# A decoder layer's second MLP product with its operands prepared two pairs to an instruction, and work moved between the vector engines

## The chip, the cores and the metric

The kernel runs on one core of a Trainium2 chip. The metric is the device time of one execution in microseconds. The core's engines are TensorE (PE in the profile; its weight loads are PEld), VectorE (DVE), ScalarE (ACT), GpSimd (POOL) and SyncE (SP), which here only issues transfers. Each takes its instructions in order and waits on semaphores for the others.

## The reference

One hybrid decoder layer, for 2048 tokens of width 1024, in float32:

```python
h = rmsnorm(x, g_mix);  z = h @ w_in
y_a = rwkv7_mix(token_shift(z[..., :RWKV_COLS]), ...) @ w_out_a
y_b = multiscale_pool_mix(z_pool, ...) @ w_out_b
x = x + (sigmoid(gA) * y_a + sigmoid(gB) * y_b) @ w_o
h = rmsnorm(x, g_mlp)
x = x + square(relu(h @ w_ff1)) @ w_ff2            # 1024 -> 4096 -> 1024
h = rmsnorm(x, g_ple)
x = x + sigmoid(h @ w_ple_gate) * (p @ w_ple_proj)
out = rmsnorm(x, g_final)
```

## The kernel before

The stages follow one another: the mixing stage (0 to 1690 us of the profile), the MLP's first product (1690 to 2390), its second (2390 to 3037), and the gate stage (3037 to the end).

A float32 operand is split for TensorE (`split`): ScalarE casts it to a rounded form, the high part, and DVE or POOL subtracts that from it, which leaves the low part. A product of two split operands is three matmuls (`mm3`: high by high, high by low, low by high). Each matmul is 128x128 by 128x512.

Both MLP products work on two blocks of 1024 tokens and replace eight products of half-size operands by seven, P1 to P7, of sums and differences of the halves (a Strassen scheme in Winograd's form). The activations' combinations (A11, S2, A12, S3, S1, A22, S4) are kept as `home` operands on chip in the first product, and go through DRAM (`rD`) in between.

The first product runs over two blocks and 16 pairs of hidden blocks. `pair` is one of these: its seven products have the order P1, P6, P2, P7, P5, P4, P3, and DVE, POOL and ScalarE form the results and their relu squared in the `t2` ring (7 tiles; L1276, L1282). Between P7 and P5, `combine` prepares the next pair's weights (lines 1165 to 1192). While block 0 runs, `heads1` norms block 1's tokens, in four groups of two tiles: ScalarE's sum of squares (L160, with an output nobody reads, a junk tile of the `t2` ring), a reciprocal root by an integer guess and Newton steps on DVE (L149 to L155, operations on 128x1), the scaling on DVE (L173, `hr`), transposes on TensorE (L137), and the home operands of block 1 into DRAM. As the last pair of block 0 finishes with each home operand, `fill_home` reads block 1's in its place.

The second product runs over `seq`: two blocks, four chunks of four pairs each, seven products in the order P1, P2, P5, P6, P7, P4, P3. One product is 48 matmuls, about 11 us. While it runs, `operands` prepares the next: the activations `raw` from DRAM in one transfer of 1 MB, split pair by pair with the low parts on POOL, and the weights (`w2`, in place combinations for P5, P6, P7 and P4 on POOL, split with the low parts on DVE). Operand tiles come from one ring: 16 tiles, two products' worth. Each product's results are added from PSUM into accumulators `accs` (ScalarE copies the first, L1440; DVE adds the others, L1442); in a block's last chunk DVE forms the outputs from them (L1448, L1460), and they are stored to `x2D`. At the block's first chunk the accumulators P2, P4 and P3 start from `x1D`.

The gate stage begins with the split of its weights (`weights`, tiles `wg`). Its first two tokens' norms (`norm_in`) are in the program near the end of the second product; the scheduler puts them where their rows are ready.

TensorE's order is written by hand. The order on the other engines is the scheduler's, from priorities that follow the program's order. SP's queue carries nearly all transfers.

## Time and profile before

| | us |
|---|---|
| median of 3 runs | 3304.99 (3300.75 to 3310.25) |
| the profiled execution | 3303.2 |
| its span | 3301.4 |
| mean granted clock of TensorE | 0.967 |
| TensorE busy | 3054.8 (93%) |
| VectorE busy | 2455.9 (74%) |
| GpSimd busy | 1653.8 (50%) |
| ScalarE busy | 1336.2 (40%) |

A busy engine is not always the one that sets the end; what matters is what it waited for. In the rows of the trace, `a<-b` is output from input, the time in brackets is TensorE's idle time before the instruction with the engine, tile and line that ended it, and a row with `x24 | 30.4, 1275 |` has a count, a busy time in us and a mean in ns.

### The profile page before, as it was taken

To read this page: it belongs to the slowest core of one execution; us is meant where nothing else is said; L and a number is where in the kernel's file an instruction comes from. 1 tells how busy PE (TensorE), PEld (TensorE's weight loads), DVE (VectorE), ACT (ScalarE), POOL (GpSimd) and SP (SyncE) were. 2 spreads that over 40 slices of the span, in tenths; PEclk is the share of its full clock that TensorE was granted. 3 is DMA by queue.
4 is the path that set the end of the run, shared out by engine and by line. 5 is a ranking of instruction groups with operands and counts; after the bars stand their busy time and mean duration, and the time that the engine had idled before them with its cause. 6 is when DMAs were issued, how large, how long until landed. Compare 5 with 4: busy or idle time off the path is not lost. (4 is left out here: it accounts for less than half of the span.)

```text
span 3301.4 us, 44294 instructions
## 1 busy us (share of the span) xinstructions
PE 3054.8 (93%) x14409; PEld 2492.0 (75%) x14409; DVE 2455.9 (74%) x5424; ACT 1336.2 (40%) x2774; POOL 1653.8 (50%) x1657
## 2 busy tenths in 40 slices
PE   7999989999999998788989889899989998999998
PEld 6777777777878786677777667688878886887787
DVE  4479888788888878875477777776657697668665
ACT  4445655455455444432233223222244434443332
POOL 4545444444334434531245456655589887885000
PEclk9999999999999999899999999899999999999999
DMA  7876767765666567767755455544464464335331
GB/s 246 241 225 196 244 202 233 237 216 192 216 211 218 188 205 238 246 213 264 273 193 177 148 177 190 181 153 147 169 227 153 142 217 177 141 128 177 127 115 67
DMA packets 423219, 636.41 MB, mean 193 GB/s; under 512 B 174222, under 2 KB 286412, under 8 KB 391756
## 3 DMA queue, kind: packets, MB, share of 16 engines
q1 hardware_dynamic: 420684, 629.39, 57.7%
q10 hardware_dynamic: 2304, 4.20, 0.3%
q8 instruction: 114, 1.87, 0.2%
q14 instruction: 117, 0.96, 0.1%
HBM read 439.49 MB, written 193.99 MB: 192 GB/s over the span
## 5 line engine op out<-in xcount | busy, mean ns | idle before, releaser
L133 PE MATMUL d<-big,wf 128*128 128x512 f32 (+1 forms) x3288 | 849.7, 406 | 19.1 <-DVE wf L244 8.9
L133 PEld LDWEIGHTS d<-big,wf 128*128 128x128 f32 x3288 | 609.5, 192 | 157.7 <-DVE wf L244 11.4
L1103 DVE TENSOR_TENSOR op<-w,op 128x512 fp32r<-128x512 f32 x224 | 287.4, 1295 | 139.2 <-ACT op L1102 137.8
L1103 POOL TENSOR_TENSOR op<-hr,op 128x512 fp32r<-128x512 f32 x224 | 331.2, 1494 | 95.5 <-ACT op L1102 95.5
L133 PE MATMUL d<-op 128*128 128x512 f32 x1344 | 314.6, 393 | 12.6 <-POOL op L1103 8.9
L133 PEld LDWEIGHTS d<-op 128*128 128x128 f32 x1344 | 253.4, 189 | 69.2 <-POOL op L1103 9.3
L1102 ACT CAST op<-hr 128x512 fp32r<-128x512 f32 x224 | 139.3, 622 | 323.2 <-PE rc L133 109.8
L872 DVE TENSOR_TENSOR Xtmp<-Xt,At 128x16 f32<-128x16 f32 (+15 forms) x512 | 242.8, 474 | 9.3
L1103 POOL TENSOR_TENSOR op<-wr,op 128x512 fp32r<-128x512 f32 x96 | 141.5, 1483 | 206.3 <-ACT op L1102 206.3
L133 PE MATMUL d<-yx,wf 128*128 128x512 f32 x768 | 206.9, 416 | 22.7 <-ACT yx L390 15.7
L133 PE MATMUL d<-wf,big 128*128 128x512 f32 x768 | 200.8, 415 | 26.1 <-DVE t2k L611 13.8
L133 PE MATMUL d<-wg,op 128*128 128x512 f32 x768 | 187.0, 399 | 11.3 <-ACT wg L1102 11.0
L133 PEld LDWEIGHTS d<-wf,big 128*128 128x128 f32 x768 | 146.6, 196 | 64.1 <-DVE t2k L611 17.4
L1276 POOL TENSOR_TENSOR t<-t,t 128x512 f32<-128x512 f32 x128 | 189.4, 1490 | 9.8 <-issue 5.6
L133 PEld LDWEIGHTS d<-yx,wf 128*128 128x128 f32 x768 | 147.3, 198 | 59.8 <-ACT yx L390 17.4
L133 PE MATMUL rp<-op 128*128 128x512 f32 x672 | 173.5, 393 | 13.9 <-DVE accP L1442 12.3
L133 PEld LDWEIGHTS d<-wg,op 128*128 128x128 f32 x768 | 147.1, 192 | 46.4 <-ACT wg L1102 11.6
L1102 ACT CAST op<-wr 128x512 fp32r<-128x512 f32 x192 | 110.0, 618 | 166.9 <-DMA wr<-in_w_ff_dram 113.1
L133 PE MATMUL rc<-op 128*128 128x512 f32 x672 | 171.7, 391 | 0.0
L244 POOL TENSOR_TENSOR wf<-wr,wf 128x640 fp32r<-128x640 f32 (+2 forms) x69 | 120.5, 1747 | 78.5 <-ACT wf L241 74.3
L133 PEld LDWEIGHTS rp<-op 128*128 128x128 f32 x672 | 126.9, 190 | 42.0 <-issue 12.7
L875 DVE TENSOR_REDUCE Xt<-Xtmp 128x8 f32<-128x16 f32 (+15 forms) x512 | 147.3, 288 | 9.2
(319 smaller groups left out, 6396.4 us busy)
## 6 DMA issues: line engine op xcount, KB each, us to landing
wf<-wc SPq DMA_DIRECT2D x131, 1024.0 KB, 5.4
wc<-wf SPq DMA_DIRECT2D x50, 1024.0 KB, 6.3
wr<-in_w_ff_dram SPq DMA_DIRECT2D x64, 512.0 KB, 4.4
w<-in_w_ff_dram SPq DMA_DIRECT2D x64, 512.0 KB, 4.2
wr<-in_w_in_dram SPq DMA_DIRECT2D x51, 512.0 KB, 4.3
zD<-t2k SPq DMA_DIRECT2D x96, 256.0 KB, 3.9
zs<-zD SPq DMA_DIRECT2D x32, 640.0 KB, 6.4
At<-aD SPq DMA_DIRECT2D x32, 512.0 KB, 5.1
```

The lines of the kernel that those rows point to most:

```text
L133: PE.matmul(out_, lhsT, rhs, start=start, stop=stop, **kw)
L244: eng.tensor_tensor(wf[:, 1, c], raw[:, c], hi.bitcast(F32)[:, c], ALU.subtract)
L872: DVE.tensor_tensor(tmp[:, :, :, 0:n], Xt[:, :, 0:n].unsqueeze(2).broadcast_to([P, MCOL, FS, n]), At[:, 0:n, r:n].rearrange("p s r -> p r ...
L875: DVE.tensor_reduce(Xt[:, :, r:n].unsqueeze(3), tmp[:, :, :, 0:n], AX.X, ALU.add)
L1102: ACT.copy(out=dst[0], in_=src)
L1103: eng.tensor_tensor(dst[1], src, dst[0].bitcast(F32), ALU.subtract)
L1276: eng.tensor_tensor(out_, a, b, op)
```

## The change

- The operand ring has tiles of twice the size, half as many. In the first product each is handed out in halves (`ophalf`).
- In the second product two pairs share an instruction: two casts and two low parts for the activations of a product instead of four each, two and two for the weights. Of the activations' low parts the first stays on POOL and the second is DVE's. The weight combinations go from POOL to DVE. The weights come in transfers of 1 MB instead of 512 KB.
- In the first product P7's weight difference goes from POOL to DVE.
- Block 1's norms take their squares in halves of 512 into a tile of their own, with an added 128x1 sum on DVE; the other norms are as before.
- `fill_home` gets high priority, and its low parts are 1024 and 512 wide on DVE and 512 wide on POOL instead of 1024 on each.
- P4's and P3's accumulators are loaded at P6 instead of P1; the last block's stores go from ScalarE's queue to SP's; the gate stage's first two weight transfers are issued one product before the end.

```diff
--- before.py
+++ after.py
@@ -1085,15 +1085,24 @@
             return t
 
         gb = gvec(g_mlp[0])
-        ring = dict(n=0, a=6, b=6)
+        ring = dict(n=0, a=3, b=3)
 
         def optile():
 
             n = ring["n"] % (ring["a"] + ring["b"])
             ring["n"] += 1
             if n < ring["a"]:
-                return hx.tile([P, 2, 512], FR, name="op", tag="op", bufs=ring["a"])
-            return ring["pool"].tile([P, 2, 512], FR, name="op", tag="op", bufs=ring["b"])
+                return hx.tile([P, 2, 2, 512], FR, name="op", tag="op", bufs=ring["a"])
+            return ring["pool"].tile([P, 2, 2, 512], FR, name="op", tag="op", bufs=ring["b"])
+
+        half = []
+
+        def ophalf():
+
+            if not half:
+                t = optile().rearrange("p s x (k n) -> p s x k n", n=P)
+                half.extend((t[:, 0, x], t[:, 1, x]) for x in range(2))
+            return half.pop(0)
 
         def hr(shape=(P, 4, 512)):
             return hx.tile(list(shape), F32, name="hr", tag="hr", bufs=2)
@@ -1106,7 +1115,15 @@
 
             for e, x_ in enumerate(xt):
                 SP.dma_start(out=x_, in_=x1D[blk * TC + e * 512 + j * P:blk * TC + e * 512 + (j + 1) * P, :])
-                norm_tile(pool, x_, gb, x_, junk)
+                if junk:
+                    norm_tile(pool, x_, gb, x_, junk)
+                    continue
+                ss = pool.tile([P, 2], F32, name="nss2", bufs=2)
+                for n in range(2):
+                    jk = pool.tile([P, 512], BF16, name="jk", bufs=1)
+                    ACT.activation(out=jk, in_=x_[:, n * 512:(n + 1) * 512], func=AF.Square, accum_out=ss[:, n:n + 1])
+                DVE.tensor_tensor(ss[:, 0:1], ss[:, 0:1], ss[:, 1:2], ALU.add)
+                DVE.scalar_tensor_tensor(x_, x_, rstd(pool, ss[:, 0:1], 1, "n"), gb, op0=ALU.mult, op1=ALU.mult)
             return xt
 
         def head(blk, j, xt, tmp, pss):
@@ -1172,9 +1189,8 @@
             ops = {}
 
             def op(nm, src, eng):
-                t = optile().rearrange("p s (k n) -> p s k n", n=P)
-                split((t[:, 0], t[:, 1]), src, eng)
-                ops[nm] = t
+                ops[nm] = ophalf()
+                split(ops[nm], src, eng)
             op("P1", b11, DVE)
             op("P2", b21, POOL)
             DVE.tensor_tensor(b11, b12, b11, ALU.subtract)
@@ -1182,7 +1198,7 @@
             t2 = tmp().rearrange("p (k n) -> p k n", n=P)
             DVE.tensor_tensor(t2, b22, b11, ALU.subtract)
             op("P6", t2, DVE)
-            POOL.tensor_tensor(b12, b22, b12, ALU.subtract)
+            DVE.tensor_tensor(b12, b22, b12, ALU.subtract)
             op("P7", b12, POOL)
             DVE.tensor_tensor(b21, b21, t2, ALU.subtract)
             op("P4", b21, DVE)
...
@@ -1249,8 +1264,9 @@
     def fill_home(nm):
 
         raw = hraws.pop(nm)
-        for k, eng in ((slice(0, 2), DVE), (slice(2, 4), POOL)):
-            split((home[nm][:, 0, k, :], home[nm][:, 1, k, :]), raw[:, k, :], eng)
+        with tc.high_priority():
+            for k, eng in ((slice(0, 2), DVE), (slice(2, 3), DVE), (slice(3, 4), POOL)):
+                split((home[nm][:, 0, k, :], home[nm][:, 1, k, :]), raw[:, k, :], eng)
         n = USE.index(nm) + 2
         if n < len(USE):
             load_home(USE[n])
@@ -1267,7 +1283,7 @@
         ps = pps()
         h = home[FIRST[nm]]
         for k in range(4):
-            mm3(ps, (ops[nm][:, 0, k, :], ops[nm][:, 1, k, :]), (h[:, 0, k, :], h[:, 1, k, :]), k == 0, k == 3)
+            mm3(ps, (ops[nm][0][:, k, :], ops[nm][1][:, k, :]), (h[:, 0, k, :], h[:, 1, k, :]), k == 0, k == 3)
         if last:
             fill_home(FIRST[nm])
         return ps
@@ -1309,7 +1325,7 @@
     def heads1():
         for j in range(4):
             t = hr((P, 2, D))
-            xt = normed(1, j, f2, [t[:, 0, :], t[:, 1, :]], dict(tag="t2", bufs=NT2))
+            xt = normed(1, j, f2, [t[:, 0, :], t[:, 1, :]], None)
             yield
             hd = head(1, j, xt, tmp2, (dps, dps))
             next(hd)
@@ -1342,16 +1358,17 @@
     c3 = ExitStack()
     g3 = c3.enter_context(tc.tile_pool(name="g3", bufs=1, side="right", reuse_waits="tile"))
     f3 = c3.enter_context(tc.tile_pool(name="f3", bufs=1, side="left", reuse_waits="tile"))
-    ring.update(pool=f3, b=10, n=0)
-    w2v = w_ff2[0].rearrange("(k p) c -> p k c", p=P)
+    ring.update(pool=f3, b=5, n=0)
+    w2v = w_ff2[0].rearrange("(q x e p) c -> p q e x c", x=2, e=2, p=P)
     lo, hi = slice(0, 512), slice(512, D)
 
     def load_w2(c):
+
         w = {}
         for e in range(2):
-            for p_ in range(KC):
-                w[p_, e] = g3.tile([P, D], F32, name="w2", tag="w2", bufs=12)
-                SP.dma_start(out=w[p_, e], in_=w2v[:, 2 * (c * KC + p_) + e, :])
+            for q in range(KC // 2):
+                w[q, e] = g3.tile([P, 2, D], F32, name="w2", tag="w2", bufs=6)
+                SP.dma_start(out=w[q, e], in_=w2v[:, c * KC // 2 + q, e])
         return w
 
     w2 = {0: load_w2(0)}
@@ -1366,28 +1383,35 @@
         raw = hr()
         SP.dma_start(out=raw, in_=rD[blk][FIRST[nm]][:, c * KC:(c + 1) * KC, :])
         res = []
-        for p_ in range(KC):
+        for q in range(KC // 2):
             a = optile()
-            split((a[:, 0, :], a[:, 1, :]), raw[:, p_, :], POOL)
-            e, o = w[p_, 0], w[p_, 1]
-            b11, b12, b21, b22 = e[:, lo], e[:, hi], o[:, lo], o[:, hi]
+            split((a[:, 0], a[:, 1]), raw[:, 2 * q:2 * q + 2, :], (POOL, DVE)[q])
+            e, o = w[q, 0], w[q, 1]
+            b11, b12, b21, b22 = e[:, :, lo], e[:, :, hi], o[:, :, lo], o[:, :, hi]
             if nm == "P5":
-                POOL.tensor_tensor(b11, b12, b11, ALU.subtract)
+                DVE.tensor_tensor(b11, b12, b11, ALU.subtract)
             elif nm == "P6":
-                POOL.tensor_tensor(b11, b22, b11, ALU.subtract)
+                DVE.tensor_tensor(b11, b22, b11, ALU.subtract)
             elif nm == "P7":
-                POOL.tensor_tensor(b12, b22, b12, ALU.subtract)
+                DVE.tensor_tensor(b12, b22, b12, ALU.subtract)
             elif nm == "P4":
-                POOL.tensor_tensor(b21, b21, b11, ALU.subtract)
+                DVE.tensor_tensor(b21, b21, b11, ALU.subtract)
             b = optile()
-            split((b[:, 0, :], b[:, 1, :]), dict(P1=b11, P2=b21, P5=b11, P6=b11, P7=b12, P4=b21, P3=b22)[nm], DVE)
-            res.append((a, b))
+            split((b[:, 0], b[:, 1]), dict(P1=b11, P2=b21, P5=b11, P6=b11, P7=b12, P4=b21, P3=b22)[nm], DVE)
+            res += [(a[:, :, x], b[:, :, x]) for x in range(2)]
         return res
 
     def rows_of(blk, e, j):
         return slice(blk * TC + e * 512 + j * P, blk * TC + e * 512 + (j + 1) * P)
 
-    hts, xts = {}, {}
+    wgv = w_ple_gate[0].rearrange("(k p) c -> p k c", p=P)
+    wpv = w_ple_proj[0].rearrange("(k p) c -> p k c", p=P)
+    hts, xts, graws = {}, {}, []
+
+    def raw_weights(view, n, ks):
+        raw = hr()
+        SP.dma_start(out=raw[:, 0:len(ks), :], in_=view[:, ks[0]:ks[-1] + 1, (lo, hi)[n]])
+        return raw
 
     def norm_in(j, pool, bufs):
 
@@ -1398,8 +1422,8 @@
     def turn_in(j, ps):
 
         xt = xts.pop(j)
-        hts[j] = ht = [hx.tile([P, 2, 512], FR, name="op", tag="op", bufs=ring["a"]).rearrange(
-            "p s (k t) -> p (s k) t", t=P) for _ in range(2)]
+        ht = hx.tile([P, 2, 2, 512], FR, name="op", tag="op", bufs=ring["a"])
+        hts[j] = ht = [ht[:, s_].rearrange("p x (k t) -> p (x k) t", t=P) for s_ in range(2)]
         for h in range(2):
             pt = ps()
             for k in range(4):
@@ -1412,12 +1436,11 @@
     for n, (blk, c, nm) in enumerate(seq):
         cur = nxt
         g = blk * NCH + c
-        if nm == "P1":
-            if c == 0:
-
-                for a, e, ns in (("P2", 0, lo), ("P4", 1, lo), ("P3", 0, hi)):
-                    for j in range(4):
-                        SP.dma_start(out=accs[a][j], in_=x1D[rows_of(blk, e, j), ns])
+        if c == 0:
+
+            for a, e, ns in dict(P1=[("P2", 0, lo)], P6=[("P4", 1, lo), ("P3", 0, hi)]).get(nm, ()):
+                for j in range(4):
+                    SP.dma_start(out=accs[a][j], in_=x1D[rows_of(blk, e, j), ns])
         if nm == "P5" and g + 1 < NBLK * NCH:
             w2[g + 1] = load_w2((g + 1) % NCH)
         final = c + 1 == NCH
@@ -1427,6 +1450,8 @@
 
                 ring["n"] = 0 if n + 3 == len(seq) else ring["a"]
             nxt = operands(b_, c_, nm_, w2[b_ * NCH + c_])
+        if n + 2 == len(seq):
+            graws += [raw_weights(wgv, 0, ks) for ks in (range(4), range(4, 8))]
         pss = [dps() for _ in range(4)] if n % 2 == 0 else [rps(), rps(), cps(), cps()]
         for p_, (a, b) in enumerate(cur):
             if n + 1 == len(seq) and p_ >= 2:
@@ -1448,7 +1473,7 @@
                 DVE.tensor_tensor(s[to], s[a], s[b], ALU.add)
 
             def put(k, e, ns):
-                (ACT if blk + 1 == NBLK else SP).dma_start(out=x2D[rows_of(blk, e, j), ns], in_=s[k])
+                SP.dma_start(out=x2D[rows_of(blk, e, j), ns], in_=s[k])
             if nm == "P2":
                 add("P2", "P2", "P1")
                 put("P2", 0, lo)
...
```

TensorE's instructions keep their order. Elsewhere the order moves. First ScalarE, in the first product of block 0, where a group's norm (`nss` is the sum of squares) meets the next pair's weight casts (`op<-wr`). Before:

```order
L1291 COPY t_17940<-rp 128x512
L1102 CAST op<-t_18002 128x512
L1102 CAST op<-wr 128x512 x5
L160 ACTIVATE junk,nss<-hr 128x1024 x2
L1291 COPY t_18136<-d 128x512
L1102 CAST op<-wr 128x512 x2
L1102 CAST op<-t_18198 128x512
```

Now:

```order
L1163 COPY hr<-d 128x512
L1111 CAST op<-wr 128x512
L1163 COPY hr<-d 128x512
L1124 ACTIVATE jk,nss_18065<-hr 128x512
L1163 COPY t_17889<-d 128x512
L1124 ACTIVATE jk,nss_18065<-hr 128x512
L1307 COPY t_17929<-rp 128x512
L1124 ACTIVATE jk,nss_18090<-hr 128x512 x2
L1111 CAST op<-t_17989 128x512
L1111 CAST op<-wr 128x512 x6
```

The squares (L160, now L1124) stand right behind the transposes' copies, ahead of six weight casts instead of after five.

Then ScalarE at the start of the second product, where it casts activations (`hr`) and weights (`w2`). Before, with P1's operands from `op_22474` to `op_22495`, P2's after them:

```order
L1102 CAST op_22474<-hr_22472 128x512
L1291 COPY t2_22311<-d_22298 128x512
L1102 CAST op_22477<-w2_22428 128x512
L1102 CAST op_22480<-hr_22472 128x512
L1102 CAST op_22483<-w2_22430 128x512
L1102 CAST op_22486<-hr_22472 128x512
L1102 CAST op_22489<-w2_22432 128x512
L1102 CAST op_22492<-hr_22472 128x512
L1102 CAST op_22495<-w2_22434 128x512
L1102 CAST op_22512<-hr_22510 128x512
L1102 CAST op_22515<-w2_22436 128x512
L1102 CAST op_22518<-hr_22510 128x512
```

Now, with P1's operands `op_22392`, `op_22395`, `op_22398` and `op_22401`, P2's `op_22410` to `op_22419`, and P5's first pairs `op_22480` and `op_22484`:

```order
L1111 CAST op_22392<-hr_22390 128x1024
L1307 COPY t2_22237<-d_22224 128x512
L1111 CAST op_22395<-w2_22354 128x1024
L1111 CAST op_22398<-hr_22390 128x1024
L1111 CAST op_22480<-hr_22478 128x1024
L1111 CAST op_22484<-w2_22354 128x1024
L1111 CAST op_22401<-w2_22356 128x1024
L1111 CAST op_22410<-hr_22408 128x1024
L1111 CAST op_22413<-w2_22358 128x1024
L1111 CAST op_22416<-hr_22408 128x1024
```

P5's first two casts stand between P1's last two.

Last, DVE at the boundary of the two blocks in the second product, where the first norm of the gate stage (L149 to L165) stands. Before:

```order
L1103 TENSOR_TENSOR op<-w_24518,op 128x512
L1448 TENSOR_TENSOR accP_22470<-accP_22470,accP_22446 128x512
L1448 TENSOR_TENSOR accP_22471<-accP_22471,accP_22447 128x512
L1103 TENSOR_TENSOR op<-w_24504,op 128x512
L1103 TENSOR_TENSOR op<-w_24506,op 128x512
L165 TENSOR_SCALAR nmsn<-nss 128x1
L149 TENSOR_SCALAR rs_yn<-nmsn 128x1
L151 TENSOR_SCALAR rs_hn<-nmsn 128x1
L150 TENSOR_SCALAR rs_yn<-rs_yn 128x1
L153 TENSOR_TENSOR rs_qn<-rs_yn 128x1
L154 TENSOR_TENSOR rs_qn<-rs_qn,rs_hn 128x1
L155 SCALAR_TENSOR_TENSOR rs_yn<-rs_qn,rs_yn 128x1
```

Now:

```order
L1112 TENSOR_TENSOR op<-hr,op 128x1024
L1394 TENSOR_TENSOR w_24084<-w_24088,w_24084 128x2x512
L1112 TENSOR_TENSOR op<-w_24086,op 128x1024
L1398 TENSOR_TENSOR w_24088<-w_24088,w_24084 128x2x512
L1394 TENSOR_TENSOR w_24086<-w_24090,w_24086 128x2x512
L1398 TENSOR_TENSOR w_24090<-w_24090,w_24086 128x2x512
L1112 TENSOR_TENSOR op<-w_24084,op 128x1024
L165 TENSOR_SCALAR nmsn<-nss 128x1
L1467 TENSOR_TENSOR accP_22366<-accP_22366,rp 128x512
L1467 TENSOR_TENSOR accP_22367<-accP_22367,rp 128x512
L149 TENSOR_SCALAR rs_yn<-nmsn 128x1
L151 TENSOR_SCALAR rs_hn<-nmsn 128x1
```

The combinations (L1394, L1398) have come in ahead of the norm, and block 1's adds from PSUM (L1467) between its steps.

More of the change, by code (lines that the diff above doesn't have):

```diff
@@ L1237, in hybrid_kernel @@
     SP.dma_start(out=raw, in_=w1v[:, 4:8, P:2 * P])
-    t = optile().rearrange("p s (k n) -> p s k n", n=P)
-    split((t[:, 0], t[:, 1]), raw, POOL)
-    ops_next["P3"] = t
+    ops_next["P3"] = ophalf()
+    split(ops_next["P3"], raw, POOL)
     USE = ("A11", "S2", "A12", "S3", "S1", "A22", "S4")
@@ L1479, in hybrid_kernel @@
     f4 = ctx.enter_context(tc.tile_pool(name="f4", bufs=1, side="left", reuse_waits="tile"))
-    wgv = w_ple_gate[0].rearrange("(k p) c -> p k c", p=P)
-    wpv = w_ple_proj[0].rearrange("(k p) c -> p k c", p=P)
     wgs, wps, pts, xs, fss = {}, {}, {}, {}, {}
@@ L1485, in weights @@
     def weights(view, res, pool, n, ks, nm):
-        raw = hr()
-        SP.dma_start(out=raw[:, 0:len(ks), :], in_=view[:, ks[0]:ks[-1] + 1, (lo, hi)[n]])
+        raw = graws.pop(0) if graws else raw_weights(view, n, ks)
         for i, k in enumerate(ks):
```

## The prediction

> **What bounds the kernel now.** I read the page's head, then busy times by stretch, then TensorE's waits, then single waits in the order of time.
>
> ```profile
> span 3301.4 us, 44294 instructions
> PE 3054.8 (93%) x14409; PEld 2492.0 (75%) x14409; DVE 2455.9 (74%) x5424; ACT 1336.2 (40%) x2774; POOL 1653.8 (50%) x1657
> ```
>
> TensorE is the bound on the average, so only its idle time can be gained. The stretches (busy time and count on PE, PEld, DVE, ACT and POOL, then the granted clock, the DMA share and GB/s) show where that lies among the stages the change touches:
>
> ```profile
> 1740.00:1840.00 100.00, 85.28 (x366) 69.01 (x366) 77.93 (x136) 25.57 (x46) 57.83 (x39) 0.91 0.51 168
> 1900.00:1990.00 90.00, 77.73 (x340) 63.08 (x340) 64.93 (x102) 22.21 (x41) 48.37 (x33) 0.92 0.50 161
> 2040.00:2100.00 60.00, 43.16 (x150) 32.02 (x150) 54.39 (x44) 20.27 (x28) 50.62 (x27) 0.83 0.66 229
> 2100.00:2380.00 280.00, 280.00 (x1213) 227.50 (x1212) 187.99 (x252) 63.15 (x111) 160.18 (x113) 1.00 0.42 142
> 2380.00:2460.00 80.00, 69.43 (x290) 55.61 (x289) 44.38 (x38) 33.75 (x63) 65.62 (x44) 0.94 0.66 240
> 2460.00:2650.00 190.00, 190.00 (x836) 156.64 (x835) 134.64 (x141) 82.42 (x147) 169.66 (x116) 1.00 0.44 155
> 2650.00:2727.00 77.00, 77.00 (x340) 63.47 (x339) 72.70 (x80) 28.26 (x50) 61.78 (x37) 1.00 0.65 226
> 2727.00:2777.00 50.00, 34.03 (x137) 26.89 (x137) 41.17 (x50) 24.39 (x46) 33.00 (x26) 0.86 0.51 181
> 3037.00:3070.00 33.00, 20.76 (x66) 14.30 (x66) 28.39 (x63) 17.41 (x33) 14.87 (x10) 0.74 0.69 247
> ```
>
> Where nothing is missing, TensorE is busy for the whole stretch: 1213 matmuls in 280 us (4.33 per us) in the first product, 836 in 190 (4.40) in the second. There the change can gain nothing. Elsewhere the loss is the stretch less its count over that rate, which includes the lower clock after a stall: 15.5 and 11.5 us in the norms for block 1, 25.4 where the home operands are refilled, 14.1 at the second product's start, 18.9 at its block boundary, 18.0 at the gate stage's start: 103 in all. What TensorE waits for:
>
> ```profile
> PE d L137 <- DVE hr L173: 28.8, 6, 10.2
> PE d L133 <- DVE t2k L636: 13.4, 6, 9.1
> PE d L133 <- ACT wg L1102: 11.0, 2, 6.3
> PE rc L133 <- DVE big L1103: 5.4, 1, 5.4
> ```
>
> **Block 1's norms.** The two long ones of the six waits on `hr` are the second tile's of two heads:
>
> ```profile
> 1835.41 1.09 PE L137 MATMUL d<-ident,hr 128*128 128x128 f32 x4 [10.19 <-DVE hr L173]
> 1972.55 1.11 PE L137 MATMUL d<-ident,hr 128*128 128x128 f32 x4 [10.13 <-DVE hr L173]
> ACT junk L160 <- POOL t L1276: 16.1, 7, 2.9
> ```
>
> The third row is one of ScalarE's waits. A norm's reciprocal root is a chain of 128x1 steps on DVE, here from the block boundary, alone and beside POOL:
>
> ```profile
> 2737.17 0.15 DVE L154 TENSOR_TENSOR rs_qn<-rs_qn,rs_hn 128x1 f32<-128x1 f32 x1
> 2738.68 1.22 DVE L153 TENSOR_TENSOR rs_qn<-rs_yn 128x1 f32<-128x1 f32 x1
> 2739.94 1.22 DVE L154 TENSOR_TENSOR rs_qn<-rs_qn,rs_hn 128x1 f32<-128x1 f32 x1
> ```
>
> ScalarE's squares wait for a junk tile from the `t2` ring, whose slot POOL still uses, and DVE's chain starts late. With a tile of their own the squares stand ahead of most of the next pair's casts. The chain's end still stands behind other DVE work of its pair, so I leave about 4 us of each long wait and all the short ones: 20.3 - 8 = 12, and 1 for the lower clock after them: 13 gained (0 if that DVE work, not the squares, set the end; 22 if only 5 of 27 remain). The added 128x1 sum costs 0.15 to 1.2 us, eight times, under matmuls.
>
> **P7's combination on DVE.** The durations (ns: shortest, median, longest) of DVE's 512-wide operations in the second product:
>
> ```profile
> L1103 DVE TENSOR_TENSOR op<-w,op x224: 676/1293/1850, 2387.7 to 3021.7; 128x512 fp32r<-128x512 f32 x112
> ```
>
> 33 more of that size come to the first product's DVE, on an engine busy 188 of 280 us at full matmul speed: 33 x 0.68 to 1.85 us, 22 to 61 us over some 690, hidden in the 92 idle us per 280 (uncovered, each would cost its length). Only at the end of the mixing stage does TensorE wait for DVE (`t2k`): one operation there, 1 us lost (0 to 2).
>
> **Refilling the home operands.** Seven refills each move a 512-wide low part from POOL to DVE.
>
> ```profile
> L1103 DVE TENSOR_TENSOR hA<-hr,hA x2: 2283/2300/2318, 2040.9 to 2059.2; 128x1024 fp32r<-128x1024 f32 x2
> L1103 DVE TENSOR_TENSOR yx<-hr,yx x1: 1212/1212/1212, 2066.0 to 2066.0; 128x1024 fp32r<-128x1024 f32 x1
> L1103 POOL TENSOR_TENSOR big<-hr,big 128x1024 fp32r<-128x1024 f32 x2 | 6.0, 2982 | 0.1
> L1102 ACT CAST hS<-hr 128x1024 fp32r<-128x1024 f32 x4 | 4.0, 1044 | 0.0
> ```
>
> A 1024-wide DVE operation takes 1.21 us alone and 2.30 beside POOL. DVE (54.4 of 60 us busy) gets 7 x 0.68 = 4.8 us more; POOL loses half of such a 3-us operation per refill, some 10, and what DVE loses beside it falls by about as much as DVE gets. So the load does not change the time; putting the refills ahead of the pair's other work does. Bounds: -2, and +16 if nearly two thirds of 25.4 go. I take +6, near the low end, since DVE stays full.
>
> **The second product's operands.** Rows of block 0's last chunk (2650 to 2727), where DVE is fullest, and POOL's form over the whole run:
>
> ```profile
> L1103 DVE TENSOR_TENSOR op<-w,op 128x512 fp32r<-128x512 f32 x24 | 30.4, 1275 | 3.8 <-ACT op L1102 3.8
> L1448 DVE TENSOR_TENSOR accP<-accP,accP 128x512 f32<-128x512 f32 x28 | 28.5, 1046 | 0.0
> L1460 DVE TENSOR_TENSOR accP<-accP,xr 128x512 f32<-128x512 f32 x4 | 4.9, 1228 | 0.0
> L1442 DVE TENSOR_TENSOR accP<-accP,d 128x512 f32<-128x512 f32 x12 | 7.9, 675 | 1.7 <-PE d L133 1.7
> L1103 POOL TENSOR_TENSOR op<-hr,op x224: 1256/1301/1856, 2374.4 to 3014.1; 128x512 fp32r<-128x512 f32 x112
> ```
>
> Beside POOL an operation with two operands in SBUF takes 1.05 to 1.28 us instead of 0.68; one that reads PSUM stays at 0.675. The surplus, 24 x 0.595 + 28 x 0.366 + 4 x 0.55 = 27 us, came beside 37 POOL instructions: 0.7 us each, half the 1.3 us that such an instruction takes.
>
> After the change a chunk has 29 wide DVE operations (14 weight low parts, 7 of the activations, 8 combinations), 28 adds from PSUM, and in a last chunk 32 more adds: 29 x 1.21 + 28 x 0.675 + 32 x 0.68 = 75.8 us. The rows of 2650 to 2727 sum to 79.6 where DVE is busy 72.7, since operations overlap by 0.086 each; less 89 x 0.086 that is 68. POOL keeps 7 wide low parts of some 2 x 1.3 us; at 0.7 (per instruction) to 1.3 (half its length) they add 5 to 9. So 73 to 77 us of 77: as full as before, when TensorE lost nothing. An ordinary chunk: 68 - 32 x 0.6 + 5 to 9 = 54 to 58. I take 2 lost in both last chunks together (0 to 12). ScalarE's 4 wide casts (1.04) per product replace 8 narrow ones, off the path. The weight loads keep their bytes and the depth of their ring, from P5 to the next chunk's P1, which hides them:
>
> ```profile
> w<-in_w_ff_dram SPq DMA_DIRECT2D x64, 512.0 KB, 4.2
> ```
>
> Nothing, then; without that cover, about twice those 4.2 us for a load of 1 MB.
>
> At the stage's start POOL's combinations stood ahead of P1's last low parts:
>
> ```profile
> 2393.53 3.44 POOL L1375 TENSOR_TENSOR w<-w 128x512 f32<-128x512 f32 x2
> 2400.29 4.60 POOL L1379 TENSOR_TENSOR w<-w,w 128x512 f32<-128x512 f32 x3
> 2407.38 4.63 PE L133 MATMUL d<-op 128*128 128x512 f32 x10 [8.90 <-POOL op L1103]
> ```
>
> They leave POOL, but now ScalarE has P5's first two casts ahead of P1's second weight cast, and the first of them writes the buffer that P1's first half must have been read from. From that half's end: three casts at 1.04 and two low parts at 1.21, 5.5 us, up to the old 8.9 if P5's raw lands late; the first low part is also twice as wide, 1 us later. Of 14.1 I gain 4 (-1 to +8).
>
> **The block boundary.** The chains of the gate stage's first two norms (their rows are block 0's) stand on DVE among block 1's first adds, in 128x1 steps as above:
>
> ```profile
> 2759.43 2.90 PE L133 MATMUL rp<-op 128*128 128x512 f32 x6 [12.27 <-DVE accP L1442]
> ```
>
> Some 24 steps, most of them at 1.2 us, hold up the adds that empty PSUM. POOL will work 2.6 us in each 11, so most steps are short; eight of the twelve accumulator loads move to a later product, which frees their queue. I gain 16 of 18.9 (8 if half the steps still meet POOL; 19).
>
> **The gate stage's start.**
>
> ```profile
> 3041.69 8.68 PE L133 MATMUL d<-wg,op 128*128 128x512 f32 x24 [4.66 <-ACT wg L1102]
> 3058.95 5.42 PE L133 MATMUL d<-wg,op 128*128 128x512 f32 x10 [6.33 <-ACT wg L1102]
> x2D<-accP ACTq DMA_DIRECT2D x12, 256.0 KB, 2.0
> ```
>
> The stores no longer hold up ScalarE's casts, but DVE's low part still follows the last adds, and the next loads now stand behind the stores on SP. Gain 3 (-4 to +7).
>
> **Sum:** 13 - 1 + 6 - 2 + 4 + 16 + 3 = 39 us. The profiled execution took 3303.2 us, 1.8 under the median of the three runs shown: 3264, given as 3265.
>
> **Rivals.**
> Waits replaced: the norms, the refills and both stage starts keep their waits (DVE stays full in each), and the boundary alone gains: -1 - 2 + 16 = 13, so 3290. For it: DVE ended most of these waits. Against it: the squares and POOL's combinations do leave the chains. Chance 0.20.
> All waits go to their good ends: 22 + 16 + 8 + 19 + 7 = 72, so 3231. For it: DVE has idle time in every stretch but two. Chance 0.12.
> A POOL instruction shuts out DVE for its whole length: 7 x 2.6 = 18 per chunk instead of 5 to 9; a last chunk needs 86 us, 9 over, twice: 18 lost instead of 2, so 3281. Against it: 0.7 us per instruction of 1.3 to 1.7 in the rows above. Chance 0.08. The Trainium skill ("SBUF — State Buffer", Who interferes with whom) has this rule: a DVE instruction with two SBUF inputs and a GpSimd instruction that reads SBUF exclude each other, the later one blocking fully. The trace agrees on which operations suffer (the adds from PSUM do not), and shows half the price on average.
> Slower: wide operations take 2.30 us throughout, as beside the wide POOL instructions of the refills. A last chunk then needs 68 + 29 x 1.09 = 100 us (23 over, twice), each of six ordinary ones 49 + 32 = 81 (4 over), 70 in all; the boundary's gain goes too: 3303 - 25 + 70 = 3348. It turns slower from a mean of 1.95 us per wide operation, where the last chunks cost 25. POOL would have to work most of the time, and has 2.6 us in 11. Chance 0.07.
>
> **Numbers.** My forecast has the other 0.53, at 3245 to 3284. The range, 3236 to 3292, takes in the replaced waits and the lock, and leaves out most of the all-gone and the slower case. A difference within 0.3%, 10 us, is about what a measurement can tell from no change. Faster: 0.53 + 0.12 + 0.08 + half of the replaced waits 0.10 = 0.83; the same 0.10; slower 0.07.
>
> **What would show it.** Right: the 10-us waits on `hr` at half or less, 128x1 steps of 0.15 us at the boundary and no wait over 5 us there, one wait of 5 to 9 us at the second product's start with a ScalarE `op` cast or DVE as releaser, wide operations of mean 1.2 to 1.5 us. Wrong: TensorE below full busy time in the last chunks, or the waits on `hr` still at 10.

## The result and the profile after

The changed kernel takes 3266.36 us (median of 4 runs, 3263.04 to 3274.3), the kernel before 3307.38 (4 runs, 3300.75 to 3310.25): a ratio of 0.9879, 95% interval 0.9856 to 0.9902, 41 us less. The forecast was 3265.

The head of the page after:

```profile
span 3266.9 us, 43509 instructions
PE 3050.8 (93%) x14409; PEld 2490.7 (76%) x14409; DVE 2520.9 (77%) x5479; ACT 1316.8 (40%) x2573; POOL 1247.4 (38%) x1329
```

POOL lost 406 us of work and DVE got 65; TensorE's work is the same. What TensorE waits for, after, in the stretches that the change touches:

```profile
PE d L133 <- ACT op L1111: 14.3, 1, 14.3
PE d L133 <- ACT wg L1111: 7.6, 2, 6.2
PE d L133 <- DVE wg L1112: 6.7, 2, 6.5
PE d L133 <- DVE t L1292: 6.2, 1, 6.2
PE d L133 <- DVE op L1112: 4.1, 1, 4.1
PE d L137 <- DVE t L1292: 3.5, 1, 3.5
PE rp L133 <- DVE big L1112: 3.4, 1, 3.4
```

The waits on DVE's `hr` and on `accP` are gone, those at the refills have shrunk to one of 3.4 us and two under 1, and a new one of 14.3 us stands at the second product's start. By stretch (columns as in the rows of before), the norms, the refills, the second product's start, the block boundary and the gate stage's start:

```profile
1740.00:1840.00 100.00, 93.78 (x413) 76.20 (x412) 85.86 (x131) 27.64 (x51) 55.71 (x37) 0.97 0.53 174
1900.00:1990.00 90.00, 86.21 (x378) 69.71 (x377) 75.49 (x113) 25.43 (x47) 53.39 (x36) 0.98 0.61 197
2030.00:2090.00 60.00, 54.73 (x223) 42.84 (x222) 58.94 (x66) 23.67 (x38) 37.23 (x23) 0.94 0.68 239
2358.00:2430.00 72.00, 53.58 (x222) 43.11 (x221) 43.67 (x32) 27.45 (x33) 20.87 (x9) 0.86 0.64 234
2690.00:2740.00 50.00, 50.00 (x219) 40.96 (x219) 45.94 (x66) 26.75 (x35) 12.25 (x5) 1.00 0.77 269
3000.00:3036.00 36.00, 21.16 (x66) 15.36 (x67) 25.45 (x60) 13.80 (x27) 12.40 (x9) 0.72 0.72 261
```

The boundary runs at full speed, 219 matmuls in 50 us at clock 1.00, where it had 137 in 50 us at 0.86. The second product's start has lost more than before: TensorE stands idle for 18.4 of 72 us.

TensorE executes the same 14,409 matmuls in the same order in every kernel here, so one number per place says who leads: how much earlier than in the profile of before the same matmul starts, each from its own span's start. The change of this lead over a stretch is what the kernel gained there. The stretches are cut at the same matmuls in all kernels (7950 begins the first product, 9060 ends the norms, 9150 to 9450 the refills, 10500 to 10800 the start, 11700 to 12250 the boundary, 13210 to 13450 the gate stage's start).

| us gained in | mixing stage | block 1's norms | refills | second product's start | block boundary | rest of the second product | gate stage's start | span |
|---|---|---|---|---|---|---|---|---|
| forecast | -1 | 13 | 6 | 4 | 16 | -2 | 3 | 39 |
| changed kernel | -7.0 | 21.2 | 16.6 | -7.5 | 18.2 | -2.8 | -4.2 | 34.5 |
| norm_junk | -3.0 | -1.8 | 16.2 | -7.7 | 18.3 | -2.9 | -4.0 | 15.1 |
| p7_pool | -10.1 | 21.8 | 16.2 | -7.7 | 18.3 | -2.9 | -4.4 | 31.2 |
| fill_plain | -6.8 | 21.9 | 16.6 | -8.1 | 18.3 | -2.9 | -4.8 | 34.2 |
| fill_half | -0.7 | 21.9 | 12.1 | -7.4 | 18.2 | -2.8 | -3.9 | 37.4 |
| fill_half_p7 | -8.4 | 23.4 | 14.7 | -7.7 | 18.3 | -2.9 | -4.4 | 33.0 |
| combos_pool | -3.6 | 21.6 | 13.7 | -5.1 | 9.4 | -2.9 | -4.6 | 28.5 |
| acc_p1 | -3.0 | 21.9 | 16.0 | -7.5 | 18.3 | -2.9 | -4.0 | 38.8 |
| start_order | -4.4 | 21.0 | 15.6 | 7.5 | 18.3 | -2.9 | -3.9 | 51.2 |
| stores_act | -5.7 | 22.0 | 13.7 | -7.2 | 18.2 | -2.8 | -0.1 | 38.1 |
| ring_only | -9.2 | -6.0 | 13.1 | 2.0 | -0.4 | 0.0 | -0.9 | -1.3 |
| norm_only | -1.1 | 21.0 | 2.0 | 0.6 | -2.5 | 0.0 | 0.0 | 20.1 |
| best | -9.4 | 20.2 | 13.7 | 8.7 | 18.3 | -2.9 | -1.3 | 47.3 |

(Rounding leaves up to 0.2 us between a row and its span.) The mixing stage varies between -0.7 and -10.1 over kernels whose instructions there are the same up to its last 100 us, so that column is the scatter of single executions. It is negative in every row, since the profile of before was a quick one there; its -7 is why the changed kernel's profile shows 34.5 us where the medians show 41. The other columns repeat within 2.5 us wherever nothing was changed (the widest is norm_only's -2.5 at the boundary, where its instructions are those of before), except the refills, which scatter from 13.7 to 16.6. Each row is one profiled execution, and all experiments but `best` were run only once, so they are compared by these columns.

### The profile page after: what moved, and what is told of

It reads as the page before. It is cut to its first block, busy times and chain, and to the rows that moved or that the text cites. A ratio compares the mean times of both kernels' runs of the same rounds, so it can differ in the third digit from the quotient of the medians.

```text
span 3266.9 us, 43509 instructions
## 1 busy us (share of the span) xinstructions
PE 3050.8 (93%) x14409; PEld 2490.7 (76%) x14409; DVE 2520.9 (77%) x5479; ACT 1316.8 (40%) x2573; POOL 1247.4 (38%) x1329
## 5 line engine op out<-in xcount | busy, mean ns | idle before, releaser
L133 PE MATMUL d<-op 128*128 128x512 f32 x1344 | 318.6, 396 | 18.4 <-ACT op L1111 14.3
L1112 POOL TENSOR_TENSOR op<-hr,op 128x1024 fp32r<-128x1024 f32 x56 | 154.9, 2766 | 457.2 <-ACT op L1111 457.2
L133 PEld LDWEIGHTS d<-op 128*128 128x128 f32 x1344 | 254.3, 189 | 77.8 <-ACT op L1111 14.7
L1112 DVE TENSOR_TENSOR op<-w,op 128x1024 fp32r<-128x1024 f32 x112 | 183.6, 1641 | 107.4 <-ACT op L1111 107.4
L1111 ACT CAST op<-hr 128x1024 fp32r<-128x1024 f32 x112 | 117.7, 1051 | 358.8 <-issue 156.2
L1112 POOL TENSOR_TENSOR op<-wr,op 128x512 fp32r<-128x512 f32 x96 | 153.1, 1598 | 251.0 <-ACT op L1111 243.1
```

The lines of the kernel that those rows point to most:

```text
L133: PE.matmul(out_, lhsT, rhs, start=start, stop=stop, **kw)
L1111: ACT.copy(out=dst[0], in_=src)
L1112: eng.tensor_tensor(dst[1], src, dst[0].bitcast(F32), ALU.subtract)
```

## The experiments

**norm_junk**: in `heads1` of the changed kernel

```diff
-            xt = normed(1, j, f2, [t[:, 0, :], t[:, 1, :]], None)
+            xt = normed(1, j, f2, [t[:, 0, :], t[:, 1, :]], dict(tag="t2", bufs=NT2))
```

> The changed kernel with one part undone: block 1's norms take their squares 1024 wide again, with the junk tile of the t2 ring. Place measured: how far the same TensorE matmul lies ahead of the kernel before, from the first product's start to the end of block 1's norms (21 us gained there by the change). Theory: the junk tile made the squares late, so 15 to 21 us of it are lost again and TensorE has two waits of about 10 us on hr. Rival: POOL has less to do since P7's differences left it, the t2 ring is free sooner, and the junk tile no longer matters: under 6 us lost, no wait over 4 us.

3288.14 us in its one run, and 23 us lost in the norms alone (21.2 to -1.8). TensorE's waits there are back, with four on `hr`, and so is ScalarE's on the junk tile (its waits of TensorE, then single ones in order of time, then its waits of ScalarE):

```profile
PE d L137 <- DVE hr L173: 28.1, 4, 9.7
```

```profile
1771.44 1.12 PE L137 MATMUL d<-ident,hr 128*128 128x128 f32 x4 [9.71 <-DVE hr L173]
1910.15 1.11 PE L137 MATMUL d<-ident,hr 128*128 128x128 f32 x4 [9.22 <-DVE hr L173]
```

```profile
ACT junk L160 <- POOL t L1292: 15.6, 6, 4.7
```

The last row is the mechanism: the squares wait for POOL to finish with the `t2` slot that their unread output needs. In the changed kernel the same view has the squares (`jk`) waiting only for their rows to land. ScalarE's wait for POOL's adds has not vanished; it stands at the copies of P1's results into `t2` tiles (L1307):

```profile
ACT t L1307 <- POOL t L1292: 18.5, 6, 4.7
ACT jk L1124 <- DMA hr<-x1D: 17.0, 7, 4.1
```

This run undoes the tile of their own and the halving of the squares together; which of the two the gain needs was not tried apart.

**p7_pool**: `combine`'s line for P7 back on POOL.

```diff
-            DVE.tensor_tensor(b12, b22, b12, ALU.subtract)
+            POOL.tensor_tensor(b12, b22, b12, ALU.subtract)
```

> The changed kernel with P7's weight difference in the first product back on POOL, all else as changed. Theory (the squares' tile alone frees the norms): under 4 us lost between the first product's start and the end of block 1's norms, and under 3 us at the refills. Rival (POOL's relief frees them): 10 us or more lost in the norms.

21.8 in the norms and 16.2 at the refills: the move did nothing that these columns can show. The theory's bound held.

**fill_plain** and **fill_half**, two ways to take the refills' part back:

```diff
-        with tc.high_priority():
-            for k, eng in ((slice(0, 2), DVE), (slice(2, 3), DVE), (slice(3, 4), POOL)):
+        for k, eng in ((slice(0, 2), DVE), (slice(2, 3), DVE), (slice(3, 4), POOL)):
...
-            for k, eng in ((slice(0, 2), DVE), (slice(2, 3), DVE), (slice(3, 4), POOL)):
+            for k, eng in ((slice(0, 2), DVE), (slice(2, 4), POOL)):
```

> The changed kernel with the refills of the home operands at ordinary priority; their low parts still 1024 and 512 wide on DVE and 512 on POOL. Place: the refills of block 1's home operands (16.6 us gained there by the change). Theory: the order gives the gain, so 11 to 17 us are lost. Rival: the shorter POOL part gives it, under 5 us lost.

> The changed kernel with the refills at high priority but split as before, 1024 wide on DVE and 1024 on POOL. Theory (order): under 5 us of the 16.6 lost. Rival (share): 11 to 17 us lost. Between the two: order and share each give part of it, and this run and the one before add up to about 17.

16.6 and 12.1. Without the high priority nothing changed: the scheduler puts every instruction in the same order with it and without, so this run is in effect a repeat of the changed kernel, and its theory failed. With the old split 12.1 remained, 1.6 below the column's scatter: 4.5 lost, under the 5 that `fill_half`'s theory allowed, but not for its reason, since `fill_plain` shows that the priority makes no order. Its rival, the split, failed. Neither the priority nor the split makes the bulk of the gain; the split may make a few us of it.

**fill_half_p7**: `fill_half` and `p7_pool` together.

> The changed kernel with two parts undone together: the refills' low parts 1024 wide on POOL again, and P7's differences in the first product on POOL. Place: the refills (16.6 us gained by the change; undoing the first alone left 12.1, the second alone 16.2). Theory: POOL's load paces the refills, since a raw buffer is free for the next load only after POOL's low part, and either relief is nearly enough; with both undone under 5 of 16.6 remain. Rival: the operand ring's new tiles or the order around the refills give it, so 10 or more remain.

14.7 remained. POOL's load does not pace the refills; the theory fell, and its rival pointed at the operand ring.

**ring_only**: the kernel before, with the double tiles handed out in halves everywhere, and nothing else of the change.

```diff
-        ring = dict(n=0, a=6, b=6)
+        ring = dict(n=0, a=3, b=3)
...
+                t = optile()
+                half.extend(t[:, :, x] for x in range(2))
...
-            a = optile()
+            a = ophalf()
```

> The kernel before with the operand ring's part of the change alone: tiles of twice the size, half as many, handed out in halves everywhere; widths, engines and transfers as before. Places: the refills (16.6 us gained by the whole change; 12 to 16 remained when the refills' own split, its priority and P7's move were undone), and the pace of TensorE in the second product (a matmul every 229.3 ns after the change, 227.7 before). Theory: the ring is what frees the refills, so 10 to 16 us are gained there. Rival: under 4 us, and what frees them is to be sought in the norms that come ahead of them. For the pace: 229 if the places of the new tiles set it, 227.7 if it comes from the wide instructions.

3304.54 us, and 13.1 us gained at the refills: the ring gives that gain by itself. It gives back 6.0 in the norms, so that the kernel as a whole did not gain. A slot now comes free only when both halves of a tile are used up, and the scheduler's order moves: DVE's rows, in program order, up to the third home operand's refill (A12, in `hA`), first of the kernel before, then of this one, whose line numbers differ:

```
L1276 TENSOR_TENSOR t_19908<-t_19865,rp 128x512
L1183 TENSOR_TENSOR t_19943<-wr 128x512
L1187 TENSOR_TENSOR wr<-wr,t_19943 128x4x128
L1103 TENSOR_TENSOR op<-t_19943,op 128x512
L1276 TENSOR_TENSOR t_19978<-t_19908,rp 128x512
L1276 TENSOR_TENSOR t_19865<-t_19865,rp 128x512
L1282 SCALAR_TENSOR_TENSOR t_19978<-t_19978 128x512
L1103 TENSOR_TENSOR hA_16378<-hr,hA_16378 128x1024
```

```
L1285 TENSOR_TENSOR t_19852<-t_19809,rp 128x512
L1192 TENSOR_TENSOR t_19886<-wr 128x512
L1196 TENSOR_TENSOR wr<-wr,t_19886 128x4x128
L1112 TENSOR_TENSOR hA_16378<-hr,hA_16378 128x1024
L1285 TENSOR_TENSOR t_19919<-t_19852,rp 128x512
L1285 TENSOR_TENSOR t_19809<-t_19809,rp 128x512
L1112 TENSOR_TENSOR op<-t_19886,op 128x512
```

The refill now stands ahead of the next pair's low part (`op<-t`) and of two adds and a relu of the running pair. In the changed kernel's trace it stands there too. That this order is what gains the 13 us, and not the tiles in another way, was not tried apart.

**norm_only**: the kernel before, with the changed kernel's `normed` and `heads1`.

> The kernel before with the norms' part of the change alone: block 1's squares in halves into a tile of their own. Places: block 1's norms and the refills. Theory: 17 to 24 us gained at the norms, as in the whole change, and under 4 us at the refills. Rival for the norms (they need POOL relieved too): under 12. Rival for the refills: the norms' earlier end frees them, and 10 or more are gained there too.

3283.12 us: 21.0 in the norms, 2.0 at the refills. The norms' part needs nothing else of the change, and gives nothing else beyond the scatter.

**combos_pool**: the four combinations of `operands` on POOL, 1024 wide.

```diff
-                DVE.tensor_tensor(b11, b12, b11, ALU.subtract)
+                POOL.tensor_tensor(b11, b12, b11, ALU.subtract)
...
```

> The changed kernel with the weight combinations of the second product back on POOL, 1024 wide as the change has them. Place: the block boundary (17 us gained there by the change, measured as how far the same TensorE matmul lies ahead of the kernel before). Theory: POOL's work beside the 128x1 steps made the boundary's wait, so 8 to 17 us are lost there, and the 128x1 steps at the boundary take about 1.2 us each again. Rival: the later loads of P4's and P3's accumulators and the norm's place in DVE's order give it, so under 4 us are lost. DVE has 8 wide operations less per chunk, so the last chunks have no reason to lose time by either theory.

9.4 of 18.2 us remained at the boundary: 8.8 lost, at the low end of the 8 to 17 of the theory. Some 128x1 steps were slow again, and slower than before the change (DVE in this kernel, then POOL beside it, then TensorE's wait):

```profile
2713.42 0.16 DVE L154 TENSOR_TENSOR rs_qn<-rs_qn,rs_hn 128x1 f32<-128x1 f32 x1
2713.62 2.26 DVE L155 SCALAR_TENSOR_TENSOR rs_yn<-rs_qn,rs_yn 128x1 f32<-128x1 f32 x1
2715.92 2.33 DVE L153 TENSOR_TENSOR rs_qn<-rs_yn 128x1 f32<-128x1 f32 x1
2718.28 2.28 DVE L154 TENSOR_TENSOR rs_qn<-rs_qn,rs_hn 128x1 f32<-128x1 f32 x1
2715.82 4.73 POOL L1112 TENSOR_TENSOR op<-hr,op 128x1024 fp32r<-128x1024 f32 x2
2724.68 2.90 PE L133 MATMUL rp<-op 128*128 128x512 f32 x6 [5.78 <-DVE accP L1467]
```

Beside POOL instructions of 2.4 us (4.73 for two) a step takes 2.3, where it took 1.2 beside those of 1.3 us. Fewer steps met one, though: four of 18, where 15 of 18 took 1 us or more before. The steps with two inputs by group, in this kernel (2705 to 2732):

```profile
L153 DVE TENSOR_TENSOR rs_qn<-rs_yn 128x1 f32<-128x1 f32 x6 | 5.0, 830 | 0.1
L154 DVE TENSOR_TENSOR rs_qn<-rs_qn,rs_hn 128x1 f32<-128x1 f32 x6 | 3.1, 510 | 0.1
L155 DVE SCALAR_TENSOR_TENSOR rs_yn<-rs_qn,rs_yn 128x1 f32<-128x1 f32 x6 | 3.0, 508 | 0.1
```

That is 11.1 us for 18 steps.

**acc_p1**: all twelve accumulator loads at P1 again.

```diff
-            for a, e, ns in dict(P1=[("P2", 0, lo)], P6=[("P4", 1, lo), ("P3", 0, hi)]).get(nm, ()):
+            for a, e, ns in dict(P1=[("P2", 0, lo), ("P4", 1, lo), ("P3", 0, hi)]).get(nm, ()):
```

> The changed kernel with all twelve accumulator loads of a block issued at P1 again. Place: the block boundary (17 us gained by the change; with the combinations back on POOL 8.7 of it remained). Theory: what remained there comes from DVE's order, where block 1's adds now stand between the norm's steps, so under 3 us are lost. Rival: it comes from the loads, since the first adds of P2 wait for accumulators behind eight others on SP's queue, so 5 to 9 us are lost. Second place: the second product's start, where eight transfers of 256 KB come back ahead of P5's raw: by 2 MB at the about 400 GB/s that the transfer engines moved there, the wait of 14.3 us there grows by up to 5 us.

18.3 at the boundary and -7.5 at the start, with a wait of 14.33 us there: with the combinations on DVE the loads' place costs nothing at either. So the loads are an unlikely source of what combos_pool left of the boundary's gain. Two candidates remain, and were not tried apart. One is DVE's new order, with the adds from PSUM between the norm's steps. The other is the rest of POOL's relief: half of the activations' low parts stay on DVE in combos_pool.

**start_order**: one edge in ScalarE's order. `cast[0]` is the last cast that `split` traced; at n = 1 that is P2's last.

```diff
+            cast[0] = ACT.copy(out=dst[0], in_=src)
...
+            with tc.issue_after(cast[0].ins) if n == 1 else ExitStack():
+                nxt = operands(b_, c_, nm_, w2[b_ * NCH + c_])
```

> The changed kernel with one ordering edge: ScalarE takes P5's first casts at the second product's start only after P2's last cast. Place: the second product's start (10 us lost there by the change at its worst, with TensorE waits of 14.3 and 4.1 us). Theory (order): P1's second half no longer stands behind P5's raw transfer, both waits fall to under 3 us together, and 14 to 20 us come back, about 3250 in all. Rival (transfers): the second half's weights and P2's operands land late too, since the transfer engines are full there, so TensorE waits elsewhere for over 10 us and less than 6 come back.

3252.03 us; the start gains 7.5 instead of losing 7.5. What ScalarE waited for shows in the changed kernel in the order of time, with DVE's low parts behind it, stretched beside POOL, and TensorE's two waits:

```profile
2375.77 1.04 ACT L1111 CAST op<-hr 128x1024 fp32r<-128x1024 f32 x1 [18.45 <-DMA hr<-rD0S]
2377.79 5.83 DVE L1112 TENSOR_TENSOR op<-w,op 128x1024 fp32r<-128x1024 f32 x2 [11.66 <-ACT op L1111]
2378.76 0.80 PE L133 MATMUL d<-op 128*128 128x512 f32 x1 [14.30 <-ACT op L1111]
2383.67 7.94 PE L133 MATMUL d<-op 128*128 128x512 f32 x23 [4.12 <-DVE op L1112]
```

And the one wait that start_order has left there, 0.7 us over the 3 that its theory allowed:

```profile
2367.02 8.18 PE L133 MATMUL d<-op 128*128 128x512 f32 x23 [3.72 <-DVE op L1114]
```

P5's raw transfer landed at 2375.7, and the cast of P1's second half came behind it. Its weights had long been there: start_order's cast of them, held up by nothing but their landing, began at 2356.67.

**stores_act**: the last block's stores on ScalarE's queue again.

```diff
-                SP.dma_start(out=x2D[rows_of(blk, e, j), ns], in_=s[k])
+                (ACT if blk + 1 == NBLK else SP).dma_start(out=x2D[rows_of(blk, e, j), ns], in_=s[k])
```

> The changed kernel with the last block's stores on ScalarE's queue again. Place: the gate stage's start (4.2 us lost there by the change). Theory: the stores now hold up SP's next loads, so 3 to 6 us come back. Rival: the loss is DVE's, whose last adds meet POOL's early low parts of the gate's weights, and with the stores on ScalarE the casts are late again as before: between 3 us more lost and 2 gained.

4.1 us came back at the gate stage's start. In the changed kernel the stores hold SP's queue until 3004.9, and POOL's early low parts stretch DVE's last adds, which the first gate weight on DVE must follow:

```profile
2990.00 14.90 SPq L1476 DMA_DIRECT2D x2D<-accP  x8
2997.52 5.88 POOL L1112 TENSOR_TENSOR wg<-hr,wg 128x512 fp32r<-128x512 f32 x4 [20.58 <-ACT wg L1111]
3000.50 4.05 DVE L1473 TENSOR_TENSOR accP<-accP,accP 128x512 f32<-128x512 f32 x3
3005.21 7.73 PE L133 MATMUL d<-wg,op 128*128 128x512 f32 x23 [6.48 <-DVE wg L1112]
```

Three adds took 4.05 us (1.89 before the change). With the stores back on ScalarE its casts are late again, and so POOL starts after the adds: the wait was 4.67 instead of 6.48. Both causes go with this one edit, so the run does not tell them apart. The lead does in part: about 2 of the changed kernel's 4.2 us are lost by the matmuls behind that wait, and the rest behind a second wait, for a cast that itself waited for a gate weight to land:

```profile
3029.05 0.50 PE L133 MATMUL d<-wg,op 128*128 128x512 f32 x1 [1.42 <-ACT wg L1111]
```

**best**: `start_order` and `stores_act` together.

> The changed kernel with the ordering edge of P5's first casts behind P2's last, and with the last block's stores on ScalarE's queue. Theory: the two act at different places and add up, 15 + 4 us below the changed kernel's 3266, so 3245 to 3251, 0.980 to 0.984 of the kernel before. Rival: the stores on ScalarE's queue meet the earlier casts and the gate stage takes its 4 us back, 3250 to 3254.

3248.25 us (median of 5 runs, 3245.82 to 3255.92) against 3310.36 (9 runs): a ratio of 0.9808, interval 0.9790 to 0.9827, wholly below the changed kernel's 0.9856 to 0.9902. The two gains add up but for 1.2 us at the gate stage's start, and this version is the fastest here.

## Why the prediction was right, and where its terms were off

The total was right, 39 us forecast and 41 measured, but by terms that were off on both sides: the norms (+8), the refills (+11) and the boundary (+2) gave more, the second product's start (-11.5) and the gate stage's start (-7) less. That these errors cancel to 2 us is luck, and no sign that each term was understood.

- **What bounds the kernel.** Held, with one exception. Nothing was gained where TensorE had been busy throughout, and every gain lies in the stretches named. But 2.8 us were lost in the rest of the second product, where TensorE stays busy and its matmuls only follow one another more slowly (last section); the sum had no term for that.
- **Norms, 13 (0 to 22): 21.2.** The mechanism was right and stands alone (norm_only). The mis-sized step was "I leave about 4 us of each long wait and all the short ones": 6.2 and 3.5 us were left in all, and on adds (`t`), none on `hr`.
- **P7's combination, hidden.** Held: p7_pool moves no column. It is 32 operations, not the 33 of the forecast (5479 on DVE after, 5447 in p7_pool). The 1 us at the end of the mixing stage is within that column's scatter.
- **Refills, 6 (-2 to 16): 16.6.** The step that failed is "putting the refills ahead of the pair's other work does": the high priority, from which this order was to come, changes none at all. The order did move, but through the ring, which gains 13.1 by itself and for which the sum had no term. Whether the order is how the ring gains it stays open.
- **The last chunks, -2: no wait.** TensorE is busy for 77 of 77 us, and DVE for 70.3, where 73 to 77 was forecast. (The table's -2.8 is the slower matmuls, another cause.) Block 0's last chunk after, first as a stretch, then DVE's weight low parts, activation low parts, two of the combinations' groups and the adds:

```profile
2610.00:2687.00 77.00, 77.00 (x338) 63.14 (x337) 70.32 (x78) 27.99 (x28) 24.34 (x8) 1.00 0.55 192
```

```profile
L1112 DVE TENSOR_TENSOR op<-w,op 128x1024 fp32r<-128x1024 f32 x13 | 18.5, 1423 | 6.2 <-ACT op L1111 6.2
L1112 DVE TENSOR_TENSOR op<-hr,op 128x1024 fp32r<-128x1024 f32 x7 | 10.1, 1443 | 0.4 <-ACT op L1111 0.4
L1398 DVE TENSOR_TENSOR w<-w,w 128x1024 f32<-128x1024 f32 x2 | 4.5, 2260 | 0.0
L1396 DVE TENSOR_TENSOR w<-w,w 128x1024 f32<-128x1024 f32 x1 | 3.3, 3315 | 0.0
L1473 DVE TENSOR_TENSOR accP<-accP,accP 128x512 f32<-128x512 f32 x20 | 15.3, 790 | 0.0
```

  The weight low parts took 1.42 us on the mean. All 26 wide operations, with three combinations of 3.6 us in all that are not shown, took 40.0 us, a mean of 1.54: just above the 1.2 to 1.5 forecast, and under the 1.95 from which the slower rival begins. The rival of the full lock asked for 86 us of DVE in 77, and did not come.
- **Second product's start, 4 (-1 to 8): -7.5.** The order of the casts was seen and the wait named, with its releaser. The price failed at "up to the old 8.9 if P5's raw lands late": 8.9 was the length of another wait, no bound for a transfer of which no row was shown. It came to 14.3 and 4.1 us, where one wait of 5 to 9 was forecast.
- **Boundary, 16 (8 to 19): 18.2.** Held, and no wait is left there. The 128x1 steps with two inputs by group, of the changed kernel (2700 to 2740; its 3.0 us hold one step that met a POOL instruction), then of before (2727 to 2765):

```profile
L153 DVE TENSOR_TENSOR rs_qn<-rs_yn 128x1 f32<-128x1 f32 x6 | 3.0, 523 | 0.0
L155 DVE SCALAR_TENSOR_TENSOR rs_yn<-rs_qn,rs_yn 128x1 f32<-128x1 f32 x6 | 0.8, 157 | 0.0
L154 DVE TENSOR_TENSOR rs_qn<-rs_qn,rs_hn 128x1 f32<-128x1 f32 x6 | 0.8, 155 | 0.0
```

```profile
L155 DVE SCALAR_TENSOR_TENSOR rs_yn<-rs_qn,rs_yn 128x1 f32<-128x1 f32 x6 | 7.3, 1218 | 0.2
L154 DVE TENSOR_TENSOR rs_qn<-rs_qn,rs_hn 128x1 f32<-128x1 f32 x6 | 6.2, 1026 | 0.2
L153 DVE TENSOR_TENSOR rs_qn<-rs_yn 128x1 f32<-128x1 f32 x6 | 6.0, 1001 | 0.2
```

  It is 18 steps that POOL stretches, not some 24: the eight with one input took 0.15 us each before the change too. These 18 took 19.5 us before, 11.1 in combos_pool and 4.6 after, while the boundary's gain is 0, 9.4 and 18.2: the two go together. combos_pool gives the combinations' move to DVE about half of the gain; what the other half is remains open (acc_p1).
- **Gate stage's start, 3 (-4 to 7): -4.2.** The step "the stores no longer hold up ScalarE's casts" was right, but not followed to what the earlier casts set off: POOL's low parts beside DVE's last adds, where about 2 us are lost. The loads behind the stores on SP were named and not priced above the gain; whether they are the later 2 us is not shown.

The Trainium skill ("SBUF — State Buffer", Who interferes with whom) says that a DVE and a GpSimd instruction that both need the shared read port exclude each other for a whole instruction. combos_pool agrees as to the single step: 2.3 us beside POOL instructions of 2.4, 1.2 beside those of 1.3. For a stream of operations the price was lower. In the last chunk above, DVE's 26 wide operations took 40.0 us and the 24 adds from SBUF 19.7 (four of them, of `xr`, are not shown). That is an estimated 12 us over their times alone, 26 x 1.21 and 24 x 0.68, beside POOL's 24.3 us of work: about half, which is why the rule's rival lost.

## What to carry to other kernels

An instruction that only discards its output can still hold up a chain through the ring from which that output's tile is taken; give it a tile of its own, and look first at the rings that another engine empties late. Where a scheduler orders the queues, read its order after each edit: here a hint of high priority moved nothing, a ring of larger tiles moved the refills, and a cast that waited for a transfer, placed ahead of one whose data were there, cost 15 us. A wait on a transfer that stands ahead of ready work in a queue is priced by when the transfer lands, not by the length of the wait that it replaces.

## What the runs showed of the hardware

- A 128x1 step of DVE with two operands in SBUF that meets POOL's work waits for about one POOL instruction, at both lengths seen: 0.15 us alone, 1.2 beside 512-wide ones, 2.3 beside 1024-wide ones. Merging POOL's work into wider instructions made each step that met one slower.
- In the second product a matmul starts every 229.3 ns after the change and every 227.7 before (means over 900 matmuls without a wait, at a granted clock of 1.00 in both), 0.7%, or about 2.9 us by the table. ring_only keeps 227.7 and combos_pool 229.3, so neither the double tiles nor the engine of the combinations sets it; whether it is the two-pair instructions, the 1 MB transfers or something else of the change was not tried.
